# W_2's product of a 1-core transformer block, swept stage by stage over both column pairs, with its operands in a ring of four places on GpSimd's queue

## The chip, the core and the metric

One Trainium2 chip; the kernel is one program on one of its cores. The metric is the device time of one execution in microseconds. A core has TensorE (PE; its weight loads are shown as PEld), VectorE (DVE), ScalarE (ACT), GpSimd (POOL) and SyncE (SP), which issues DMAs from its queue. Matmuls read their operands from SBUF and write to PSUM; the large arrays lie in DRAM.

## What is computed

One transformer layer on 512 tokens of width 2048, in float32: an input layer norm, a combined projection, pooling and stick-breaking attention, an output projection with a residual and a layer norm, then the part that the change is about:

```python
h = layer_norm(DEEPNORM_ALPHA * h + mix, ln1_g, ln1_b)
f = jnp.einsum('bsd,df->bsf', h, w_ff1) + b_ff1        # 512 x 2048 by 2048 x 8192
f = jnp.square(jax.nn.relu(f))
f = jnp.einsum('bsf,fd->bsd', f, w_ff2) + b_ff2        # 512 x 8192 by 8192 x 2048
h = layer_norm(DEEPNORM_ALPHA * h + f, ln2_g, ln2_b)
```

## The kernel before, in words

Each float32 product is made of three fast matmuls: an operand is split into a high part (a cast) and a low part (operand minus high part), and `three` (L286) adds high by high, high by low and low by high in one PSUM bank.

**Phase 1, W_1's product.** It runs over 16 blocks of 512 columns of d_ff (`product`, L198). A block has eight groups; for each, `weights` (L191) loads 512 KB of W_1 on SP's queue and `parts_of` (L179) forms the high and low parts, on ACT and DVE, a half at a time in four places. A group is 24 matmuls, a block 192. The product comes out in four PSUM banks. `operands` (L684) takes them: ACT adds the bias and applies relu (r), DVE squares into g (L692), and three more DVE steps make sums (L696). The second product uses Strassen's scheme in Winograd's form, and its seven left operands, A11, A12, A22 and S1 to S4, are these sums of quarters of the block. One cast (L700) makes all seven high parts, one subtraction (L701) the seven low parts, and two writes of 1792 KB on SP's queue (L703) store them in DRAM (fh_d, fl_d), in rows of 2 KB. One place holds the high parts, one the low parts.

**Phase 2, W_2's product.** It has 4 slices (NS) of 4 blocks (PER). `load_ops` (L716) loads a slice's seven operands, high and low, 1 MB each, 14 MB in all, on SP's queue into 14 places of the pool left. W_2 is read in units of 512 KB (`w2_unit`, L727; a ring of five), and `parts` (L734) forms the parts of a unit or of a sum of units in a ring of three. `columns` (L756) does the seven products of one slice for one pair of column quarters n and n + 2: stage 1 is A11 by b11 into banks x, and S1 by c = b12 - b11 into banks v; stage 2 is S2 and S4 by b22 - c and b22; stage 3 is S3 by b22 - b12; stage 4 is A12 and A22 by b21 and b21 - c. A stage runs over four units u, and a product of one unit is 12 matmuls (`times`, L741). After each stage `accumulate` (L749) adds the banks into acc, where the residual and the bias already stand. So a slice is 7 x 4 x 2 x 12 = 672 matmuls: n = 0 with all its stages, then n = 1. In the last half slice A22's product comes last, behind `between`, which loads the last layer norm's vectors into old operand places and normalises the first two of the four row blocks (`norm_out`, L821); the other two follow at the end.

The order on each engine comes from a list scheduler, which places instructions of a `high_priority` region some steps ahead; loads and parts stand in such regions.

## Time and profile before

| | us |
|---|---|
| runs (median, lowest, highest) | 2037.07, 2036.92, 2039.73 |
| the profiled execution, its own time | 2033.09 |
| its span | 2031.4 |
| TensorE busy, share of the span | 1934.5, 95% |
| DVE busy | 1238.1, 61% |
| ACT busy | 766.3, 38% |
| POOL busy | 25.6, 1% |

The span is that of the instructions of one execution. A wait is idle time of an engine, put down to what released it. The granted clock is that of TensorE as a share of its full speed of 2.4 GHz; 0.5 is its lower level, 1.2 GHz. GB/s is what the core's 16 DMA engines moved, and the DMA share is the mean busy share of these. The last two phases of the program are W_1's product (to about 1326 us) and W_2's (from there to 2004 us).

### The profile page before, as it was taken

Reading aid. Unit: us, or ns where it says so; the run is one execution under the profiler, and the core shown is the slowest. Engines: PE = TensorE matmul, PEld = TensorE weight load, DVE = VectorE, ACT = ScalarE, POOL = GpSimd, SP = SyncE. Lnnn points to the kernel's source line nnn. Section 1 sums busy time; section 2 is a strip of 40 time slices with the busy share of each in tenths; the row PEclk is TensorE's granted clock in tenths of the full one; section 3 lists DMA queues with packets and bytes.
Section 4 is the critical chain, followed back from the end, with each engine's and each line's share of the span. In section 5 each row is a group of like instructions: output and inputs, shape, how many; then the busy total and the mean of one; then the engine's idle time right before and its main releaser. Section 6 shows DMA issues by size and latency. Waiting matters only on the chain.

```text
span 2031.4 us, 22728 instructions
## 1 busy us (share of the span) xinstructions
PE 1934.5 (95%) x8736; PEld 1594.1 (78%) x8736; DVE 1238.1 (61%) x1697; ACT 766.3 (38%) x1082; POOL 25.6 (1%) x42
## 2 busy tenths in 40 slices
PE   5999999999999999999999999938999999999994
PEld 4888888888889888888888888826788788778773
DVE  8445565775469444544444544435877777877878
ACT  3354655642234233333333333322333333333331
POOL 5000000000000000000000000000000000000000
PEclk9999999999999999999999999968999999999997
DMA  5132222235344354565544565477596587587552
GB/s 218 32 94 74 82 86 81 74 117 184 106 148 126 138 166 166 205 208 170 172 166 166 206 207 171 141 292 288 166 357 246 176 331 266 182 311 281 178 186 83
DMA packets 170156, 358.07 MB, mean 176 GB/s; under 512 B 9792, under 2 KB 27328, under 8 KB 162496
## 3 DMA queue, kind: packets, MB, share of 16 engines
q1 hardware_dynamic: 169904, 356.55, 50.5%
q8 instruction: 68, 1.11, 0.2%
q14 instruction: 40, 0.33, 0.0%
q10 hardware_dynamic: 144, 0.07, 0.0%
HBM read 293.67 MB, written 62.91 MB: 176 GB/s over the span
## 4 chain that ended last, share of the span: by engine, by line
PE 77%; DMA 12%; DVE 9%; issue 1%; ACT 1%; SPq 0%; DVEq 0%; ACTq 0%
PE f L214 32%; PE qk L367 9%; PE x L289 7%; PE o L214 7%; DMA b<-in_w_ff_dram 6%; PE v L289 5%; PE p L214 4%; DMA b12b<-in_w_ff_dram 4%; PE o L289 3%; DVE tl L738 2%; PE v L214 2%; PE f L289 2%; PE w L289 2%; DVE acc L751 1%; DVE c L769 1%; DMA o3l<-fl_d 1%
## 5 line engine op out<-in xcount | busy, mean ns | idle before, releaser
L214 PE MATMUL f<-h1l,wh_f 128*128 128x512 f32 x960 | 373.5, 389 | 0.0
L214 PE MATMUL f<-h1h,wh_f 128*128 128x512 f32 x960 | 371.2, 389 | 0.0
L214 PE MATMUL f<-h1h,wl_f 128*128 128x512 f32 x960 | 353.8, 389 | 0.3 <-DVE wl_f L186 0.3
L186 DVE TENSOR_TENSOR wl_f<-raw_f,wh_f 128x512 fp32r<-128x512 f32 x240 | 160.2, 689 | 307.2 <-ACT wh_f L185 261.4
L185 ACT CAST wh_f<-raw_f 128x512 fp32r<-128x512 f32 x240 | 146.0, 621 | 407.7 <-PE f L214 395.1
L214 PEld LDWEIGHTS f<-h1h,wl_f 128*128 128x128 f32 x960 | 180.2, 188 | 38.0 <-DVE wl_f L186 0.7
L214 PEld LDWEIGHTS f<-h1l,wh_f 128*128 128x128 f32 x960 | 180.3, 188 | 37.4
L214 PEld LDWEIGHTS f<-h1h,wh_f 128*128 128x128 f32 x960 | 180.2, 188 | 37.3
L737 ACT CAST th<-c 128x1024 fp32r<-128x1024 f32 x96 | 101.2, 1054 | 189.2 <-PE x L289 57.2
L737 ACT CAST th<-b 128x1024 fp32r<-128x1024 f32 x96 | 101.2, 1054 | 170.9 <-PE x L289 112.5
L738 DVE TENSOR_TENSOR tl<-b,th 128x1024 fp32r<-128x1024 f32 x96 | 117.1, 1220 | 43.3 <-ACT th L737 42.9
L738 DVE TENSOR_TENSOR tl<-c,th 128x1024 fp32r<-128x1024 f32 x96 | 117.2, 1220 | 39.1 <-ACT th L737 39.0
L367 PE MATMUL qk<-hTl,wh_qk 128*128 128x512 f32 x256 | 99.8, 390 | 0.0
L367 PE MATMUL qk<-hTh,wh_qk 128*128 128x512 f32 x256 | 99.5, 390 | 0.0
L367 PE MATMUL qk<-hTh,wl_qk 128*128 128x512 f32 x256 | 98.8, 390 | 0.0
L701 DVE TENSOR_TENSOR fl<-g,fh 128x3584 fp32r<-128x3584 f32 x16 | 62.3, 3893 | 40.2 <-ACT fh L700 40.2
L186 DVE TENSOR_TENSOR wl_qk<-raw_qk,wh_qk 128x512 fp32r<-128x512 f32 x64 | 43.9, 688 | 64.4 <-ACT wh_qk L185 62.1
L214 PE MATMUL o<-wh_o,mixl 128*128 128x512 f32 x192 | 76.0, 396 | 0.0
L214 PE MATMUL o<-wl_o,mixh 128*128 128x512 f32 x192 | 75.9, 395 | 0.0
L289 PE MATMUL x<-th,o0h 128*128 128x512 f32 x128 | 46.4, 401 | 29.9 <-DMA o0h<-fh_d 28.7
L214 PE MATMUL o<-wh_o,mixh 128*128 128x512 f32 x192 | 72.9, 395 | 0.0
L769 DVE TENSOR_TENSOR c<-b,b 128x1024 f32<-128x1024 f32 x32 | 39.1, 1221 | 38.6 <-DMA b<-in_w_ff_dram 38.6
(236 smaller groups left out, 3914.9 us busy)
## 6 DMA issues: line engine op xcount, KB each, us to landing
b<-in_w_ff_dram SPq DMA_DIRECT2D x128, 512.0 KB, 5.0
raw_f<-in_w_ff_dram SPq DMA_DIRECT2D x120, 512.0 KB, 3.8
fh_d<-fh SPq DMA_DIRECT2D x16, 1792.0 KB, 6.0
fl_d<-fl SPq DMA_DIRECT2D x16, 1792.0 KB, 7.3
raw_qk<-in_w_in_dram SPq DMA_DIRECT2D x64, 256.0 KB, 2.9
b22b<-in_w_ff_dram SPq DMA_DIRECT2D x32, 512.0 KB, 4.1
b12b<-in_w_ff_dram SPq DMA_DIRECT2D x32, 512.0 KB, 4.5
raw_o<-in_w_out_dram SPq DMA_DIRECT2D x24, 512.0 KB, 3.7
```

Of the source, the lines that this page charges most:

```text
L185: nc.scalar.copy(h, raw[:, i, :])
L186: nc.vector.tensor_tensor(l, raw[:, i, :], f(h), op=ALU.subtract)
L214: mm = nc.tensor.matmul(bank, a, b, start=first and n == 0, stop=last and n == 2)
L289: mm = nc.tensor.matmul(bank, l, r, start=first and n == 0, stop=last and n == 2, skip_group_check=free)
L367: nc.tensor.matmul(bank, a, b, start=kc == 0 and n == 0, stop=kc == KC - 1 and n == 2)
L701: nc.vector.tensor_tensor(l, full, f(h), op=ALU.subtract)
L737: nc.scalar.copy(h, t)
L738: nc.vector.tensor_tensor(l, t, f(h), op=ALU.subtract)
L751: nc.vector.tensor_tensor(acc[tb0 + t][q], acc[tb0 + t][q], bank, op=ALU.add)
L769: nc.vector.tensor_tensor(c, b12, b11, op=ALU.subtract)
```

## The change

- `parts_of` forms the parts of a whole group (two rows of weights) by one cast and one subtraction, in two places instead of four of half the size. The pool of the weights, wp, now lives to the end.
- `operands` works in two halves of 128 of the 256 rows: each half has its cast, its subtraction and two writes of 896 KB in rows of 1 KB, on GpSimd's queue in place of SP's. A single place of half the size holds the high parts, another the low parts, so the second half's cast waits until the first half's write has landed.
- Operands of phase 2 are loaded on GpSimd's queue, a pair (high, low) at a time, into a ring of four places: two of the pool first, which is opened before phase 1 and lives on, and two of the pool right. The pairs come in order A11, S1, S2, S4, S3, A12, A22 and then those of the next slice.
- `slice_of` takes the place of `columns`: each stage runs over both column pairs before the next one, so an operand is used for both and then given up. Both pairs' c (eight of 512 KB) stay for the slice, banks are x0, x1, v0, v1, and raw units and parts come alternately from wp and right.
- The last layer norm's two vectors are loaded by two transfers (1 MB each) when `norm_out` is first reached in the order of the program, into places of their own; the first two row blocks' normalisation stands after all of w, ahead of A22's products. The second pair's A22 product is written a row block at a time.
- Spare loads of `resident` in an earlier part are one transfer of 512 KB in place of two of 256 KB.

```diff
-        wh, wl = [], []
-        for i in range(GK):
-            h = wp.tile([P, N], F32R, tag="wh", bufs=4, name=f"wh_{name}_{i}")
-            l = wp.tile([P, N], F32R, tag="wl", bufs=4, name=f"wl_{name}_{i}")
-            nc.scalar.copy(h, raw[:, i, :])
-            nc.vector.tensor_tensor(l, raw[:, i, :], f(h), op=ALU.subtract)
...
+        h = wp.tile([P, GK, N], F32R, tag="wh", bufs=2, name=f"wh_{name}")
+        l = wp.tile([P, GK, N], F32R, tag="wl", bufs=2, name=f"wl_{name}")
+        nc.scalar.copy(h, raw)
+        nc.vector.tensor_tensor(l, raw, f(h), op=ALU.subtract)
...
+    first = pool(ctx, "first", 2, side="right")
     staging = early.enter_context(ExitStack())
...
-        full = g[:, :OPS].rearrange("p o i t -> p o (i t)")
-        h = stage.tile([P, OPS, N], F32R, tag="h", name=f"fh{b}")
-        l = stage.tile([P, OPS, N], F32R, tag="l", name=f"fl{b}")
-        nc.scalar.copy(h, full)
-        nc.vector.tensor_tensor(l, full, f(h), op=ALU.subtract)
-        for d, t in ((fh_d, h), (fl_d, l)):
-            nc.sync.dma_start(d[b // PER][:, :, b % PER, :].rearrange("o p n -> p o n"), f(t))
+        for i in range(2):
+            full = g[:, :OPS, i, :]
+            h = stage.tile([P, OPS, H2], F32R, tag="h", name=f"fh{b}_{i}")
+            l = stage.tile([P, OPS, H2], F32R, tag="l", name=f"fl{b}_{i}")
+            nc.scalar.copy(h, full)
+            nc.vector.tensor_tensor(l, full, f(h), op=ALU.subtract)
+            for d, t in ((fh_d, h), (fl_d, l)):
+                nc.gpsimd.dma_start(d[b // PER][:, :, b % PER, i * H2:(i + 1) * H2].rearrange("o p t -> p o t"), f(t))
...
+    def operand(s, o):
+
+        pl = right if turn("op", 2) else first
+        both = []
+        for d, n in ((fh_d, "h"), (fl_d, "l")):
+            t = pl.tile([P, PER, 2, H2], F32R, tag=f"o{n}", bufs=2, name=f"o{n}{s}_{o}")
+            nc.gpsimd.dma_start(f(t), d[s][o].rearrange("p u (i t) -> p u i t", i=2))
+            both.append(t)
+        return both
...
+        raw = (right if turn("raw") else wp).tile([P, 2, N], F32, tag="raw", bufs=3, name=name)
...
+        with ahead():
+            S3 = operand(s, 5)
+        for n in range(2):
+            for u in units:
+                b, at, e = s * PER + u, f"{s}_{n}_{u}", (False, u == PER - 1)
+                with ahead():
+                    b22 = w2_unit(b, 1, n + 2, f"b22b_{at}")
+                    b12 = w2_unit(b, 0, n + 2, f"b12b_{at}")
+                    nc.vector.tensor_tensor(b22, b22, b12, op=ALU.subtract)
+                    p7 = parts(b22, f"7_{at}")
+                times(x[n], S3, u, p7, *e)
+            accumulate(x[n], 2, n + 2)
...
         if end:
...
+            for tb in range(2):
+                norm_out(tb)
+            for u in units:
+                times(x[0], A22, u, fourth(0, u), False, u == PER - 1)
+            accumulate(x[0], 2, 0)
+            p4 = [fourth(1, u) for u in units]
+            for t in range(2):
+                for u in units:
+                    times(x[1], A22, u, p4[u], False, u == PER - 1, (t,))
+                accumulate(x[1], 2, 1, (t,))
+                norm_out(2 + t)
```

How the change moves the instructions is shown at three places. A row has the line, the operation, the tiles and the semaphores that it waits on: DMAHW those of transfers from SP's queue, DMASW those from GpSimd's, the others of engines.

In a block of W_1's product, DVE's order; g, fl are the block's operands, wl_f the low parts of the next block's weights, with the group's first row in the name. Before:

```order
L696 TENSOR_TENSOR g_10036<-g_10036 128x512 [waits DVE_49] x3
L186 TENSOR_TENSOR wl_f_0_4_0_10134<-raw_f_0_4_10131,wh_f_0_4_0_10133 128x512 [waits DMAHW2_49,PE_49,Activation_49]
L701 TENSOR_TENSOR fl_10054<-g_10036,fh_10053 128x3584 [waits DMAHW4_49,Activation_49]
L186 TENSOR_TENSOR wl_f_0_4_1_10138<-raw_f_0_4_10131,wh_f_0_4_1_10137 128x512 [waits PE_49,Activation_49]
L186 TENSOR_TENSOR wl_f_0_6_0_10168<-raw_f_0_6_10165,wh_f_0_6_0_10167 128x512 [waits DMAHW3_49,PE_49,Activation_49]
```

And of the change:

```order
L691 TENSOR_TENSOR g_8255<-g_8255 128x512 [waits DVE_49] x3
L184 TENSOR_TENSOR wl_f_0_4_8351<-raw_f_0_4_8348,wh_f_0_4_8350 128x1024 [waits DMAHW2_49,PE_49,Activation_49]
L697 TENSOR_TENSOR fl_0_8273<-g_8255,fh_0_8272 128x1792 [waits DMASW3_49,Activation_49]
L184 TENSOR_TENSOR wl_f_0_6_8381<-raw_f_0_6_8378,wh_f_0_6_8380 128x1024 [waits DMAHW3_49,PE_49,Activation_49]
L697 TENSOR_TENSOR fl_1_8279<-g_8255,fh_1_8278 128x1792 [waits DMASW5_49,Activation_49]
L184 TENSOR_TENSOR wl_f_0_8_8411<-raw_f_0_8_8408,wh_f_0_8_8410 128x1024 [waits DMAHW4_49,PE_49,Activation_49]
```

The low parts are formed in two halves, and the second one waits for a write of the same block, with wl_f_0_8 behind it.

At the change of phase, SP's queue, which brings W_2's units (b) and, before, the operands (o0h is A11's high part). Before:

```order
L195 DMA raw_f_0_14_10301<-in_w_ff_dram 128x2x512 [waits DMAHW4_49,DVE_49]
L703 DMA fh_d_5845<-fh_10352 128x7x512 [waits Activation_49]
L703 DMA fl_d_5849<-fl_10353 128x7x512 [waits DVE_49]
L731 DMA b_0_0_0_10407<-in_w_ff_dram 128x2x512 [waits PE_49]
...
L722 DMA o0h_10373<-fh_d_5842 128x2048 [waits DMAHW1_49,PE_49]
L722 DMA o0l_10375<-fl_d_5846 128x2048 [waits PE_49]
```

And of the change, where the third number of a b is its unit u:

```order
L191 DMA raw_f_0_14_9590<-in_w_ff_dram 128x2x512 [waits DMAHW4_49,DVE_49]
L730 DMA b_0_0_0_9676<-in_w_ff_dram 128x2x512 [waits DMAHW5_49,DVE_49]
...
L730 DMA b_0_0_2_9754<-in_w_ff_dram 128x2x512
L852 DMA ln2g<-in_ln_g_dram 128x2048 [waits DMASW4_49,DMASW2_49,DMASW6_49,DMASW0_49,DVE_49]
L852 DMA ln2b<-in_ln_b_dram 128x2048 [waits DMASW5_49,DMASW7_49,DMASW3_49,DMASW1_49]
L730 DMA b_0_0_3_9790<-in_w_ff_dram 128x2x512 [waits DMAHW0_49,DVE_49]
```

Writes and operands have left this queue, six units stand right behind W_1's last load, and the last layer norm's vectors stand ahead of unit 3, with waits for writes on GpSimd's queue.

In the same place DVE's order in the change; tl is the low part of a unit or of a c, and TensorE's order is x0 with units 0 to 2, then v0 with units 0 to 2:

```order
L691 TENSOR_TENSOR g_9620<-g_9620 128x512 [waits DVE_49] x3
L738 TENSOR_TENSOR tl_0_0_2_9757<-b_0_0_2_9752,th_0_0_2_9756 128x1024 [waits DMAHW2_49,Activation_49]
L697 TENSOR_TENSOR fl_0_9638<-g_9620,fh_0_9637 128x1792 [waits DMASW7_49,Activation_49]
L697 TENSOR_TENSOR fl_1_9644<-g_9620,fh_1_9643 128x1792 [waits DMASW1_49,Activation_49]
L775 TENSOR_TENSOR c_0_0_9684<-b_0_0_0_9678,b_0_0_0_9676 128x1024 [waits DMAHW3_49]
L775 TENSOR_TENSOR c_0_1_9722<-b_0_0_1_9716,b_0_0_1_9714 128x1024 [waits DMAHW4_49]
```

Parts of the first three units (two of them ahead of these rows) are formed before the last block's low parts; the first c stands behind both of these.

## Rows read from the trace of the kernel before

**Rows 1.** Stretches: us; busy PE, PEld, DVE, ACT, POOL; granted clock, DMA share, GB/s.

```profile
75.00:1325.60 1250.60, 1250.31 (x5805) 1043.62 (x5803) 656.11 (x1046) 492.90 (x769) 0.00 (x0) 1.00 0.43 142
1325.60:1400.00 74.40, 34.35 (x107) 24.11 (x106) 31.43 (x30) 15.62 (x14) 0.00 (x0) 0.70 0.84 339
...
1453.20:1608.80 155.60, 154.41 (x673) 125.59 (x673) 120.01 (x116) 58.98 (x56) 0.00 (x0) 1.00 0.71 257
...
1920.20:2004.20 84.00, 78.83 (x337) 63.75 (x336) 66.58 (x79) 27.80 (x28) 0.00 (x0) 0.98 0.36 122
2004.20:2031.40 27.20, 0.16 (x1) 0.00 (x0) 23.08 (x52) 0.48 (x2) 0.00 (x0) 0.57 0.43 155
```

**Rows 2.** Waits of TensorE, after 1320 us, and in W_1's product (the last row).

```profile
PE x L289 <- DMA o0h<-fh_d: 28.7, 1, 28.7
PE x L289 <- DVE tl L738: 6.6, 7, 2.4
...
PE f L214 <- DVE wl_f L186: 0.3, 1, 0.3
```

**Rows 3.** Timeline of engines at the change of phase: start us, us, engine, line.

```profile
1324.63 2.19 ACT L689 ACTIVATE r<-f,vecT 128x512 f32<-128x512 f32 x3
1325.56 0.39 PE L214 MATMUL f<-h1h,wl_f 128*128 128x512 f32 x1
1330.18 3.18 ACT L700 CAST fh<-g 128x3584 fp32r<-128x3584 f32 x1 [3.36 <-DVE g L696]
1333.39 3.89 DVE L701 TENSOR_TENSOR fl<-g,fh 128x3584 fp32r<-128x3584 f32 x1 [3.25 <-ACT fh L700]
1337.72 5.40 SPq L731 DMA_DIRECT2D b<-in_w_ff_dram  x5
1343.22 0.50 SPq L722 DMA_DIRECT2D o0h<-fh_d  x1
1354.67 0.77 PE L289 MATMUL x<-th,o0h 128*128 128x512 f32 x1 [28.72 <-DMA o0h<-fh_d]
...
DMA to landing us min/median/max: 11.3/11.3/11.3
```

**Rows 4.** The page's groups of instructions: casts and low parts of phase 2.

```profile
L737 ACT CAST th<-b 128x1024 fp32r<-128x1024 f32 x96 | 101.2, 1054 | 170.9 <-PE x L289 112.5
L738 DVE TENSOR_TENSOR tl<-b,th 128x1024 fp32r<-128x1024 f32 x96 | 117.1, 1220 | 43.3 <-ACT th L737 42.9
L769 DVE TENSOR_TENSOR c<-b,b 128x1024 f32<-128x1024 f32 x32 | 39.1, 1221 | 38.6 <-DMA b<-in_w_ff_dram 38.6
```

**Rows 5.** ACT's timeline in a block of W_1's product, and in the next one.

```profile
1149.87 2.20 ACT L689 ACTIVATE r<-f,vecT 128x512 f32<-128x512 f32 x3 [0.28 <-PE f L214]
...
1193.39 2.20 ACT L689 ACTIVATE r<-f,vecT 128x512 f32<-128x512 f32 x3 [0.28 <-PE f L214]
```

**Rows 6.** The stretch 1355 to 1375, with the columns of rows 1.

```profile
1355.00:1375.00 20.00, 15.54 (x45) 10.53 (x45) 3.24 (x3) 2.09 (x2) 0.00 (x0) 0.76 1.02 424
```

**Rows 7.** The page's DMA issues: count, KB each, us to landing.

```profile
raw_f<-in_w_ff_dram SPq DMA_DIRECT2D x120, 512.0 KB, 3.8
fh_d<-fh SPq DMA_DIRECT2D x16, 1792.0 KB, 6.0
fl_d<-fl SPq DMA_DIRECT2D x16, 1792.0 KB, 7.3
```

**Rows 8.** DVE's timeline in the tail.

```profile
1993.02 1.28 DVE L751 TENSOR_TENSOR acc<-acc,w 128x512 f32<-128x512 f32 x2
...
2007.44 1.27 DVE L751 TENSOR_TENSOR acc<-acc,x 128x512 f32<-128x512 f32 x2
...
2010.37 5.32 DVE L829 SCALAR_TENSOR_TENSOR acc<-acc,rs_n,ln 128x512 f32<-128x512 f32 x8
```

**Rows 9.** DVE's groups from 700 to 1300 us, by form.

```profile
L186 DVE TENSOR_TENSOR wl_f<-raw_f,wh_f 128x512 fp32r<-128x512 f32 x221 | 147.7, 689 | 286.5 <-ACT wh_f L185 242.4 <-PE f L214 44.1
L701 DVE TENSOR_TENSOR fl<-g,fh 128x3584 fp32r<-128x3584 f32 x14 | 54.5, 3893 | 33.7 <-ACT fh L700 33.7
```

More of the change, by code (lines that the diff above doesn't have):

```diff
@@ L797, in columns @@
-        p4s = []
-        for u in range(PER):
-            b = s * PER + u
-            with ahead():
-                b21 = w2_unit(b, 1, n, f"b21_{s}_{n}_{u}")
-                p2 = parts(b21, f"2_{s}_{n}_{u}")
-                c = chain[u]
-                nc.vector.tensor_tensor(c, b21, c, op=ALU.subtract)
+        units = range(PER)
+        x = [pair(f"x{s}_{n}", f"x{n}") for n in range(2)]
+        v = [pair(f"v{s}_{n}", f"v{n}") for n in range(2)]
+        chain = {}
+        with ahead():
+            A11, S1 = operand(s, 0), operand(s, 3)
@@ new lines, in slice_of @@
+        with ahead():
+            S2, S4 = operand(s, 4), operand(s, 6)
+        for n in range(2):
+            for u in units:
+                b, at, e = s * PER + u, f"{s}_{n}_{u}", (False, u == PER - 1)
+                with ahead():
+                    b22 = w2_unit(b, 1, n + 2, f"b22_{at}")
+                    c = chain[n, u]
+                    nc.vector.tensor_tensor(c, b22, c, op=ALU.subtract)
+                    p6 = parts(c, f"6_{at}")
+                    p3 = parts(b22, f"3_{at}")
+                times(x[n], S2, u, p6, *e)
+                times(v[n], S4, u, p3, *e)
+            accumulate(x[n], 0, n + 2)
+            accumulate(v[n], 0, n + 2)
@@ new lines, in slice_of, with second, fourth @@
+        with ahead():
+            A12, A22 = operand(s, 1), operand(s, 2)
+        w = [pair(f"w{s}_{n}", f"v{n}") for n in range(2)]
+        def second(n, u):
+            at = f"{s}_{n}_{u}"
+            with ahead():
+                b21 = w2_unit(s * PER + u, 1, n, f"b21_{at}")
+                c = chain[n, u]
+                nc.vector.tensor_tensor(c, b21, c, op=ALU.subtract)
+                p2 = parts(b21, f"2_{at}")
+            times(w[n], A12, u, p2, u == 0, u == PER - 1)
+        def fourth(n, u):
+            with ahead():
+                return parts(chain[n, u], f"4_{s}_{n}_{u}")
@@ L805, in columns @@
+        for n in range(2):
+            for u in units:
+                second(n, u)
                 if not end:
[L806 to L807 removed]
+                    times(x[n], A22, u, fourth(n, u), False, u == PER - 1)
+            accumulate(w[n], 0, n)
             if not end:
[L809 to L810 removed]
+                accumulate(x[n], 2, n)
         if end:
[L812 to L816 removed]
```

146 lines of the change are left out of this document (50 added, 96 removed).

## The prediction

> **What bounds the kernel now.** I read the stretches first, then the waits of TensorE, then the rows around the change of phase, and last the DVE rows of the tail. In the table of stretches [rows 1] TensorE is busy 1250.31 of 1250.60 us during W_1's product and 154.41 of 155.60 in a full slice of W_2's: in both it is the bound, at a granted clock of 1.00. Three places leave it idle. From 1325.6 to 1400.0, the change of phase, it is busy 34.35 of 74.40 us at a mean clock of 0.70. The last half slice takes 84.00 us for 337 matmuls. And the last 27.20 us hold one matmul, while DVE is busy 23.08. A slice gives the price of a matmul: 155.60 / 673 = 0.231 us with its small stalls, and 0.227 without (one block of W_1, 192 matmuls, repeats after 1193.39 - 1149.87 = 43.52 us [rows 5]). So the 107 matmuls of the change of phase are 107 x 0.227 = 24.3 us of work, and 50.1 of its 74.4 us are lost.
>
> The waits say on what: one of 28.7 us on the load of the first operand, while nothing of the kind stands in W_1's product, whose only wait of TensorE is 0.3 us [rows 2]. The chain behind the 28.7 us [rows 3]: ACT evicts the last block, rounds all seven operands in one cast of 3.18 us, DVE forms the low parts in 3.89, the two 1792 KB writes go to SP's queue, then five loads of W_2, and only behind these, at 1343.22, the load of A11, which lands 11.3 us later. After it TensorE waits again and again: over 1355 to 1375 the DMA engines are at a share of 1.02 and 424 GB/s [rows 6], since 14 MB of operands and the first W_2 units arrive at once. The rest of the 50.1 us is the clock: TensorE's 34.35 busy us are 10.0 over 24.3.
>
> **The change, part by part.** I work with the profiled execution of before: 2033.09 us, of which 2031.4 are the span and 1.7 lie around it. It is 4.0 us under the median of the runs shown, 2037.07; I add those 4.0 at the end.
>
> *The change of phase.* Slice 0's A11 and S1 are now loaded on GpSimd's queue right after block 3's writes, over 500 us early, into places that phase 1 doesn't use; W_2's first six units are asked for ahead of the last block's operands. So the 28.7 us wait loses its cause. Let T be the end of the last W_1 matmul, about 1325.8 [rows 3]. The parts of the first unit are formed before T, and TensorE runs x0 with units 0 to 2: 36 x 0.227 = 8.2 us, to about T + 9. What is late next is c_0_0, S1's other factor. On DVE it stands behind fl_0 and fl_1, and fl_1 now waits until fl_0's write has landed, since the two halves share one place. Before, the cast began 4.4 us after T; two W_2 parts now stand ahead of it, so T + 5.3. Half a cast is 1.6 us, half of fl 1.95: fl_0 is written at T + 8.9. With L for the landing time of such a write, fl_1 is done at T + 10.9 + L, c_0_0 (1.2) at T + 12.1 + L, its cast (1.05) [rows 4] at T + 13.2 + L. TensorE stands idle for 4.2 + L.
>
> L is in no row: nothing of before is written from GpSimd's queue, and no write has 896 KB. Below, a 512 KB load lands in 3.8 us; above, I double fl_d's 7.3 us for 1792 KB to 14.6, because the queue is another one. I take 6.0, the landing of fh_d [rows 7], which has the same 896 rows at twice the length, as the nearest row. The Trainium skill ("DMA: Bandwidth & Descriptors", section on the anatomy of one DMA on the GpSimd path) fits 2.0 us plus the bytes over 436 GB/s, which would be an estimate of 4.1 us and make the sum 2 us lower; no row here shows that queue.
>
> So the idle time is 10.2 us. Then S1 with units 0 to 2 runs 8.2 us, and the next units are late: the two ln2 loads stand on SP's queue ahead of unit 3 and wait for fl_1's landing, near T + 11 + 2 x 6 = T + 23; they bring 2 MB, and S2 and S4 bring 4 MB at the same time, of which a W_2 unit gets a share of 424 GB/s. I take 5.5 us, between 0 (the loads get ahead) and 15 (6 MB at 424 GB/s, all of it in the way). The clock: before, it cost 10.0 over many idle stretches; I see two that remain and take 2.3, between 0 and 10.0. The start takes 0.8. In all 0.8 + 10.2 + 5.5 + 2.3 = 18.8 us are lost in place of 50.1: **-31**. From the bounds of L alone the loss is 16.6 to 27.4; with those of loads and clock it is 9 to 45, so the term reaches from -41 to -5.
>
> *Full slices.* The products are the same 672 matmuls, DVE and ACT work the same: DVE is busy 120 of 155.6 us. 3.3 us above 672 x 0.2267 = 152.3 are lost in each, and the change touches that with opposite signs: operand loads move off SP's queue, but S3's stage now asks two units, 1 MB, per 2.72 us for 8 units running, 385 GB/s, beside 4 MB of the next operands. Behind it three raw places of a kind hold back some of it. I take 0, between -2 and +5 per slice, -8 to +20 for four.
>
> *The end.* The last half slice's 84.0 us are 6.1 over 337 x 0.231 = 77.9. Its operands and parts are now all asked for in the same ring as elsewhere: -4, between 0 and -6. In the tail all of w is finished first, then 96 matmuls are left in place of 48. Before, the last w was added at 1993.02, 38.4 us ahead of the end [rows 8]. Now DVE has 25.0 us of queued work from the end of w to the addition of the last x (12 additions and statistics of 0.635 us, 7.6; five low parts of 1.22, 6.1; 16 scaling operations of 0.665, 10.6; 0.7 for the small ones), TensorE 21.8. From that addition before takes 2031.4 - 2007.44 = 24.0 us, of which 5.3 are eight scalings that now stand ahead of it: 18.6. So the end comes 43.6 us after w, 5.2 later than now, but w ends 48 x 0.227 = 10.9 earlier: **-5.5**, between -11 (DVE's queue is hidden) and 0.
>
> *Phase 1.* Fused parts save DVE and ACT some fixed cost, both well under TensorE: 0. Operand writes lie beside W_1's matmuls: 0 as long as L is short. That is the place to look at. In a block, t from its first matmul, some 1.2 us after the r row [rows 5], as at the change of phase [rows 3]: the operands g are ready near t = 6, fh_0 at 7.7, fl_0 at 9.7. Behind fl_1 on DVE stands wl_8, of which the fifth group has need at 4 x 5.44 + 0.45 = 22.2. fl_1 and wl_8 take 3.1 us, so fl_0 must have landed at t = 19.1: L may be 9.4 us. On ACT, fh_1 and wh_8 stand likewise, with more room. The spare loads of one DMA in place of two: 0, since they stand in a stretch with a DMA share of 0.43 or less.
>
> Sum: -31 - 4 - 5.5 = -40.5, so 1992.6 us by the profiled execution, and **1997** beside the median of before.
>
> **Rivals.** *Writes land late (slower).* If L passes 9.4 us, ACT and DVE hold back TensorE in each of the 15 blocks that have a product beside them, at (L - 9.4) us a block, and L - 6 us at the change of phase. The gain of 40.5 is gone where 15(L - 9.4) + (L - 6) = 40.5, at L = 11.7; at 14.6 the kernel would need 78 + 8.6 - 40.5 = 46 us more than before, 2083. For it: a block's 3584 KB now go in four writes of 1 KB rows, 3584 rows in place of 1792, on a queue that no row of before shows. Against it: fh_d's 6.0 and fl_d's 7.3 us for twice the bytes, and a DMA share of 0.43. What DVE runs in W_1's product is subtractions and products of two inputs, above all 221 of wl_f and 14 of fl in 600 us [rows 9]. The Trainium skill ("SBUF — State Buffer", the section on two separate sides) warns that a DMA from GpSimd's queue can starve, because GpSimd writes its descriptors itself and is shut out while DVE runs in a two-port mode, of which an fp32 copy is the example; by that rule this change is the wrong way round and L would grow by what DVE holds. Neither of these rows is a copy, so the trace gives it little weight. I give the rival 0.17, which is mostly the unknown queue.
>
> *W_2 starves.* The ring of four operand places, or stage 3's loads, cost 5 us or more a slice: 2015 to 2033. For it: 424 GB/s is what the trace shows at most, and 385 is near it. Against: that is only 21.8 us of a slice of 155.6, and the mean was 257 GB/s. 0.15.
>
> *The phase change hardly shortens.* If A11's early load waits for something of phase 1 after all, or the ln2 loads block SP's queue for long, 10 us remain of 31: 2018 to 2035, with the end's gain. 0.05.
>
> **How the numbers follow.** Forecast 0.60 (1984 to 2015), better than that 0.03, starved 0.15, unshortened 0.05, late writes 0.17. The change that this kernel's measurement can just tell is 0.2%, 4 us. All but the late writes end below 2033, save a part of the unshortened: faster 0.79, same 0.04, slower 0.17. The range from 1983 to 2035 leaves the late writes out, and the little below.
>
> **What would show it.** Right: TensorE's wait on the first operand is gone and its next waits are on th of c and on W_2 units; the loss around 1325 to 1380 is near 19 us; the slices stay near 155.6; the landing times on GpSimd's queue are 4 to 9 us; W_1's blocks stay 43.5 us long. Wrong: blocks longer than 43.6, with waits on wl_f or wh_f near the fifth group; or x waits on S3's parts in each slice; or TensorE's wait at the change of phase is still on an operand.

## The result, and the profile after

The changed kernel takes **2028.17 us** (median; 2023.15 to 2029.64) beside 2036.92 (2035.42 to 2039.73) of the kernel before in the same runs: a ratio of 0.995, interval 0.9934 to 0.9965. It is faster by 9 us, where 40 were forecast.

| | before | after |
|---|---|---|
| the profiled execution, its own time | 2033.09 | 2028.36 |
| its span | 2031.4 | 2026.7 |
| last W_1 matmul starts | 1325.56 | 1328.44 |
| first W_2 matmul starts | 1354.67 | 1329.07 |
| last W_2 matmul starts | 2003.97 | 2005.61 |

Taken apart, the span is shorter by 4.7 us: 2.9 later up to the last W_1 matmul, 28.5 less from there to the first W_2 matmul, **27.2 more from the first W_2 matmul to the last**, and 6.3 less behind it. So the wait that the change was aimed at is gone, and nearly all of it came back inside W_2's product.

The stretches of the kernel after, with the columns of rows 1 (us; busy PE, PEld, DVE, ACT, POOL; granted clock, DMA share, GB/s). The first two and the last answer to [rows 1], the third to [rows 6]; 1516.58 to 1678.40 is slice 1, 1721.92 and 1773.16 begin the stages 2 and 3 of slice 2, and the row of 15 us lies in slice 0's stage 3:

```profile
75.00:1328.50 1253.50, 1251.28 (x5804) 1043.98 (x5802) 639.00 (x864) 468.01 (x587) 58.90 (x64) 1.00 0.45 147
1328.50:1400.00 71.50, 50.29 (x196) 38.40 (x195) 47.75 (x47) 23.15 (x22) 6.99 (x10) 0.86 0.69 259
1355.00:1375.00 20.00, 9.53 (x33) 6.89 (x32) 6.22 (x6) 3.35 (x4) 0.00 (x0) 0.74 1.02 406
...
1516.58:1678.40 161.82, 156.75 (x674) 125.69 (x673) 119.09 (x117) 58.80 (x56) 7.34 (x14) 1.00 0.69 247
...
1721.92:1773.16 51.24, 46.52 (x193) 37.09 (x192) 30.50 (x30) 16.79 (x16) 2.10 (x4) 0.97 0.60 209
1773.16:1800.52 27.36, 23.28 (x97) 17.66 (x96) 19.18 (x20) 8.00 (x8) 1.05 (x2) 1.00 0.93 351
...
1445.00:1460.00 15.00, 13.01 (x54) 9.64 (x52) 8.07 (x10) 1.95 (x2) 0.00 (x0) 1.00 1.02 415
...
2005.50:2026.70 21.20, 0.50 (x3) 0.07 (x1) 17.30 (x37) 0.48 (x2) 0.00 (x0) 0.57 0.52 185
```

A full slice has become 161.82 us from 155.60. Stage 3 needs 27.36 us for 96 matmuls, 21.8 at 0.2267 each (a block of W_1: 43.52 / 192), with the DMA engines at a share of 0.93; in slice 0's stage 3 the share is 1.02 at 415 GB/s, the level of [rows 6]. Stage 2 of this slice takes 51.24 for 43.5.

The waits of TensorE after 1320 us, which answer to [rows 2]:

```profile
PE x L283 <- ACT th L737: 21.0, 7, 10.4
PE v L283 <- ACT th L737: 10.5, 1, 10.5
PE v L283 <- DVE tl L738: 6.9, 2, 4.7
PE x L283 <- DVE tl L738: 4.8, 9, 1.5
PE w L283 <- DVE tl L738: 0.4, 1, 0.4
```

The 28.7 us on an operand are gone. In their place are two waits of 10.4 to 10.5 us, both at the change of phase, and some 23 us on parts of W_2 units in the slices. The change of phase in the timeline of the kernel after, which answers to [rows 3]:

```profile
1328.44 0.39 PE L210 MATMUL f<-h1h,wl_f 128*128 128x512 f32 x1
...
1329.07 0.51 PE L283 MATMUL x<-th,oh 128*128 128x512 f32 x1 [0.25 <-ACT r L684]
...
1334.20 1.70 ACT L696 CAST fh<-g 128x1792 fp32r<-128x1792 f32 x1 [0.97 <-DVE g L691]
...
1338.59 0.94 POOL L699 DMA_DIRECT2D fl_d<-fl  x1 [1.46 <-DVE fl L697]
...
1344.11 2.03 DVE L697 TENSOR_TENSOR fl<-g,fh 128x1792 fp32r<-128x1792 f32 x1 [6.16 <-DMA fl_d<-fl]
1346.06 2.35 DVE L775 TENSOR_TENSOR c<-b,b 128x1024 f32<-128x1024 f32 x2
...
1348.41 1.22 PE L283 MATMUL v<-th,oh 128*128 128x512 f32 x2 [10.46 <-ACT th L737]
...
1351.69 0.34 SPq L852 DMA_DIRECT2D ln2b<-in_ln_b_dram  x1
1352.14 13.33 SPq L730 DMA_DIRECT2D b<-in_w_ff_dram  x6
...
1368.68 1.04 ACT L737 CAST th<-b 128x1024 fp32r<-128x1024 f32 x1 [13.79 <-DMA b<-in_w_ff_dram]
1369.78 1.22 PE L283 MATMUL x<-th,oh 128*128 128x512 f32 x2 [10.43 <-ACT th L737]
```

The first wait is the chain that the prediction worked out: fl_1 waits for fl_0's write, c for fl_1, S1's product for c. The second is unit 3, whose load is issued at 1352.14, behind the last layer norm's vectors. The DMA issues of the kernel after, which answer to [rows 7]:

```profile
fh_d<-fh POOLq DMA_DIRECT2D x32, 896.0 KB, 5.3
fl_d<-fl POOLq DMA_DIRECT2D x32, 896.0 KB, 5.9
oh<-fh_d POOLq DMA_DIRECT2D x28, 1024.0 KB, 7.9
...
b22b<-in_w_ff_dram SPq DMA_DIRECT2D x32, 512.0 KB, 6.3
```

Last, slice 2's stage 2, the timeline of the kernel after (the matmuls between are left out):

```profile
1730.32 0.39 PE L283 MATMUL v<-th,oh 128*128 128x512 f32 x1
...
1733.02 1.22 DVE L789 TENSOR_TENSOR c<-b,c 128x1024 f32<-128x1024 f32 x1 [8.20 <-DMA b<-in_w_ff_dram]
1734.16 1.22 DVE L738 TENSOR_TENSOR tl<-b,th 128x1024 fp32r<-128x1024 f32 x1
...
1735.43 0.80 PE L283 MATMUL v<-tl,oh 128*128 128x512 f32 x1 [4.72 <-DVE tl L738]
```

TensorE is without work from 1730.32 to 1735.43 for want of a tl. The b of that tl had landed before 1730 (its high part was cast at 1727.72). But DVE works in order, and a c for a later product, whose unit came late, stood ahead of it.

### The profile page after: what moved, and what is told of

It is laid out like the page before. It is cut to its first block, busy times and chain, and to the rows that moved or that the text cites. A ratio compares the mean times of both kernels' runs of the same rounds, so it can differ in the third digit from the quotient of the medians.

```text
span 2026.7 us, 22165 instructions
## 1 busy us (share of the span) xinstructions
PE 1940.9 (96%) x8736; PEld 1595.6 (79%) x8736; DVE 1216.1 (60%) x1513; ACT 739.4 (36%) x898; POOL 115.4 (6%) x162
## 4 chain that ended last, share of the span: by engine, by line
PE 53%; issue 23%; DVE 10%; DMA 10%; POOL 2%; ACT 1%; SPq 0%; DVEq 0%; POOLq 0%; ACTq 0%
PE f L210 9%; PE qk L361 9%; PE x L283 6%; PE o L210 6%; DMA b<-in_w_ff_dram 5%; PE p L210 4%; PE v L283 4%; DVE tl L738 4%; DMA b22b<-in_w_ff_dram 4%; PE o L283 3%; PE w L283 3%; PE f L283 2%; PE v L210 2%; POOL fh_d L699 1%; POOL fl_d L699 1%
## 5 line engine op out<-in xcount | busy, mean ns | idle before, releaser
L184 DVE TENSOR_TENSOR wl_f<-raw_f,wh_f 128x1024 fp32r<-128x1024 f32 x120 | 146.8, 1224 | 276.3 <-ACT wh_f L183 276.3
L183 ACT CAST wh_f<-raw_f 128x1024 fp32r<-128x1024 f32 x120 | 126.4, 1053 | 361.4 <-PE f L210 320.9
L283 PE MATMUL x<-th,oh 128*128 128x512 f32 x512 | 195.8, 397 | 21.2 <-ACT th L737 21.0
L283 PE MATMUL x<-tl,oh 128*128 128x512 f32 x512 | 203.9, 398 | 5.2 <-DVE tl L738 4.8
L283 PE MATMUL x<-th,ol 128*128 128x512 f32 x512 | 202.0, 394 | 0.0
L283 PEld LDWEIGHTS x<-tl,oh 128*128 128x128 f32 x512 | 96.9, 189 | 33.3 <-DVE tl L738 12.0
L283 PEld LDWEIGHTS x<-th,ol 128*128 128x128 f32 x512 | 96.9, 189 | 21.3
L283 PE MATMUL v<-th,oh 128*128 128x512 f32 x256 | 98.9, 398 | 10.5 <-ACT th L737 10.5
L283 PE MATMUL v<-tl,oh 128*128 128x512 f32 x256 | 102.3, 400 | 6.9 <-DVE tl L738 6.9
L283 PE MATMUL v<-th,ol 128*128 128x512 f32 x256 | 101.7, 397 | 0.0
```

The lines of the kernel that those rows point to most:

```text
L183: nc.scalar.copy(h, raw)
L184: nc.vector.tensor_tensor(l, raw, f(h), op=ALU.subtract)
L283: mm = nc.tensor.matmul(bank, l, r, start=first and n == 0, stop=last and n == 2, skip_group_check=free)
```

## The experiments

**How they are read.** The loss of a stage is the time from its first matmul's start to that of the next stage, less 0.2267 us for each matmul between. A stage is counted in TensorE's order by its number of matmuls in a slice (192, 192, 96 and 192). The loss is worked out from the starts in each run's one profiled execution. "Start" is slice 0's first 96 matmuls (x0 and v0 of stage 1); the other columns are sums over the four slices. The kernel before has 19.7 in the start, behind the 28.7 us wait, and 20.4 elsewhere. The runs of one kernel lie up to 14 us apart (e1_align: 2022.38 to 2036.02), so a difference of a few us between two variants tells nothing unless the intervals part.

| variant | median, us | ratio to before | start | stage 1 | stage 2 | stage 3 | stage 4 |
|---|---|---|---|---|---|---|---|
| the change | 2028.17 | 0.995 (0.9934 to 0.9965) | 26.5 | 2.0 | 11.6 | 22.4 | 4.9 |
| e1_align | 2030.06 | 0.9965 (0.9952 to 0.9979) | 27.4 | 2.3 | 5.3 | 21.4 | 4.9 |
| e5_align256 | 2032.06 | 0.9961 (0.9949 to 0.9973) | 26.3 | 4.1 | 12.5 | 25.3 | 1.3 |
| e3_chain | 2023.74 | 0.9934 (0.9916 to 0.9952) | 25.0 | 2.0 | 11.5 | 17.0 | 2.7 |
| e6_a11late | 2024.9 | 0.9926 (0.9906 to 0.9946) | 26.4 | 2.0 | 6.6 | 18.8 | 3.8 |
| e8_chain_late | 2028.8 | 0.9945 (0.9928 to 0.9961) | 26.9 | 2.0 | 4.8 | 3.8 | 26.6 |
| e12_spread | 2024.43 | 0.9934 (0.9913 to 0.9955) | 23.0 | 1.9 | 13.2 | 21.0 | 3.0 |
| e14_rows2k | 2038.22 | 1.0001 (0.9991 to 1.0011) | 25.5 | 6.6 | 12.9 | 31.5 | 4.6 |
| e17_sp_ops | 2018.11 | 0.9897 (0.9883 to 0.9911) | 25.9 | 2.0 | 2.7 | 24.6 | 3.8 |
| e4_lnlate | 2027.96 | 0.9956 (0.9942 to 0.9969) | 20.2 | 2.0 | 10.5 | 30.7 | 3.6 |
| e15_lag4 | 2033.11 | 0.9971 (0.9958 to 0.9984) | 27.3 | 1.9 | 2.7 | 35.1 | 3.6 |
| e7_all | 2029.51 | 0.9959 (0.9941 to 0.9977) | 7.8 | 15.3 | 14.3 | 13.5 | 26.6 |
| e13_all2 | 2013.39 | 0.9876 (0.9858 to 0.9894) | 8.5 | 5.9 | 24.8 | 7.2 | 15.3 |
| e16_all_lag4 | 1971.92 | 0.967 (0.9656 to 0.9683) | 6.6 | 8.5 | 0.0 | 0.6 | 0.4 |
| e16_all_lag6 | 1969.9 | 0.9658 (0.9643 to 0.9672) | 10.4 | 1.0 | 0.0 | 0.0 | 0.0 |

A stage's loss also moves where nothing in the stage was edited. In stage 2 the change and the six variants that leave its loads and its order alone (e1, e5, e3, e6, e8, e4) have 4.8 to 12.5; in stage 3 the change, e1 and e5 have 21.4 to 25.3. Most variants of the change that were expected to gain came out slower than their theory said, by up to 40 us (e7); both e16 came out over 10 us faster.

### Is it the matmuls themselves?

In the slices of the change, matmuls with operands in the two places of the pool first follow each other at 233 ns, those of the pool right at 227. As the kernel is built, first's places begin 224 bytes past a multiple of 256 bytes of a partition, right's at a multiple of 256. Four edits moved such a beginning. **e1_align** and **e5_align256** move first's places in the change, e1 by 96 bytes as here, e5 by 224 with `[P, 56]`:

```diff
+    pool(ctx, "gap", 1, side="right").tile([P, 24], F32, tag="gap", name="gap")
     first = pool(ctx, "first", 2, side="right")
```

> The change, with 96 unused bytes a partition ahead of the pool first, so that its two operand places start at a multiple of 128 bytes; now they start at 96 past one. Nothing else moves. Theory (a place that starts off 128 bytes makes each matmul that takes its stationary operand from it slower, 233 ns from start to start in place of 227): all of W_2's matmuls run at 227 ns, about 1340 of 2688 gain 6.7 ns each, 9 us, so near 2019 us. Rival (the slow matmuls go with the side, the queue or the time at which the place is loaded): 233 ns stays for the operands of first, and the time stays near 2028.

> The change, with 224 unused bytes a partition ahead of the pool first, so that its two operand places start at a multiple of 256 bytes. In the run with a multiple of 128, which is not one of 256, the operands of first stayed at 233 ns a matmul; the fast places of both kernels start at multiples of 256. Theory (multiple of 256 is what counts): the matmuls with operands of first fall to 227 ns, 9 us of TensorE's time in all, of which some goes into waits, so 2019 to 2025. Rival (it is where the pool lies, above 192 KB): they stay at 233 and the time at 2028.

e1 (a multiple of 128 but not of 256) still has 11.16 us per 48 matmuls with first's operands, 232.5 ns: the theory of 128 bytes falls. e5 (a multiple of 256) has 227. The same piece, three quarters of slice 2's stage 2 (144 matmuls), in the stretches of the change:

```profile
1739.56:1773.16 33.60, 33.60 (x145) 27.02 (x144) 21.84 (x21) 12.60 (x12) 1.05 (x2) 1.00 0.51 165
```

And of e5:

```profile
1739.99:1772.63 32.64, 32.64 (x146) 27.04 (x144) 20.73 (x20) 12.66 (x12) 1.05 (x2) 1.00 0.56 186
```

33.60 / 144 is 233.3 ns, 32.64 / 144 is 226.7. **e2_shift** is the converse, in the kernel before: all operands of phase 2 move by 32 bytes (and the tiles that lie behind them by 128).

```diff
+    pool(late, "gap0", 1).tile([P, 8], F32, tag="gap0", name="gap0")
     left = pool(late, "left", 1)
+    pool(late, "gap1", 1).tile([P, 24], F32, tag="gap1", name="gap1")
     right = pool(late, "right", 1)
```

> The kernel before, with its 14 operand places moved up by 32 bytes a partition, and all other tiles of phase 2 kept at multiples of 128. Theory of the start address: all 2688 matmuls of W_2's product go from 227 to 233 ns, so 18 us more than before, some 2055. Rival (the address has no part): unchanged, 2037.

Its matmuls go to 233.3 ns, and its median is 2045.8, a ratio of 1.0047 (1.0031 to 1.0064). 2688 matmuls by 6.6 ns are 17.7 us, and the small waits of a slice gave way for part of them: slice 1 takes 157.4 us, of which 156.8 are 672 x 0.2333. **e11_before_slots** moves, in the kernel before, a pool of the earlier part from 64 past a multiple of 256 to a multiple; in it lie the stationary tiles of the output projection and those of W_1's block 0:

```diff
+    slots.tile([P, 48], F32, name="gap_s")
```

> The kernel before, with 192 unused bytes a partition in the pool slots, so that the tiles of the earlier part that follow start at multiples of 256 bytes instead of 64 past one. Nothing else. Theory of the start address: the matmuls of the output projection, at 231 to 235 ns from about 440 to 625 us, fall to 227, so 4 to 5 us less: some 2032 against 2037. Rival: no change.

The last W_1 matmul starts at 1322.64, 2.9 us earlier, the median is 2034.91 and the ratio 0.9984 (0.9975 to 0.9993). The output projection's 768 matmuls go from 233.3 to 226.8 ns, 5.0 us less. But the 384 of block 0, which have 256 columns, go the other way, from 113.8 to 119.8 ns, 2.3 us more. So the effect is real, though not one rule for every shape. And it isn't what costs in the change: e5 has every matmul of W_2 at 227 and is no faster. The 9 us that it saves (half of the 2688 matmuls, 6.6 ns each) are waits in its profiled execution: by the table it loses 69.5 us in all, the change 67.4.

### Is it the bandwidth of stage 3?

**e3_chain** forms b22 - b12 as c - b11, since c = b22 - (b12 - b11) lies in SBUF already: one unit is loaded per product in place of two.

```diff
-                    b22 = w2_unit(b, 1, n + 2, f"b22b_{at}")
-                    b12 = w2_unit(b, 0, n + 2, f"b12b_{at}")
-                    nc.vector.tensor_tensor(b22, b22, b12, op=ALU.subtract)
...
+                    b11 = w2_unit(b, 0, n, f"b11b_{at}")
+                    nc.vector.tensor_tensor(b11, chain[n, u], b11, op=ALU.subtract)
```

> The change, with stage 3's factor b22 - b12 formed as c - b11, c being what stage 2 leaves (b22 - b12 + b11): one unit of 512 KB is loaded for it in place of two, 16 MB less in all, with as many DVE and ACT operations. Theory (the stalls of TensorE in stage 3, some 5 to 7 us a slice, are its loads, 1 MB for 2.72 us of matmuls, that meet 4 MB of operand loads at the limit of the DMA engines): stage 3 loses under 1.5 us a slice, 18 us less in all, near 2010. Rival (the stalls come from the ring of three raw places or the parts' ring, whatever the bytes): under 6 us gained, over 2022.

**e6_a11late** holds the load of the next slice's A11 until this slice's stage 3 has ended:

```diff
-            A11, S1 = operand(s, 0), operand(s, 3)
+            A11, S1 = operand(s, 0, ended.get(3)), operand(s, 3)
```

> The change, with the load of the next slice's A11 held back until the last matmul of stage 3. Theory (stage 3 asks 8.4 MB of units and 4.2 MB of operands, 577 GB/s over its 21.8 us, where 424 is what the DMA engines have given): with 2.1 MB less the stalls there fall from 5 to 7 us a slice to 2 to 4, so some 2017 to 2022. Rival (the stalls are the ring of raw places): no change there.

**e8_chain_late** has both edits.

> Both edits on stage 3 together: its factor formed as c - b11, with one unit in place of two, and the next A11 held back until its end. Theory: 4.2 + 2.1 MB in 21.8 us, 289 GB/s; stage 3 loses under 1 us a slice above the 233 ns matmuls, so some 2010 to 2015. Rival: a stall of 3 us or more a slice is left, from the burst of A22's load or the ring, near 2020.

e3 and e6 each take some us out of stage 3 (22.4 to 17.0 and 18.8), though neither total can be told from the change's; together, in e8, they leave 3.8. So stage 3 does ask for more than comes: less data, or the same data a little later, and its loss goes. But e8's total is that of the change, since each of the first three stages 4 now loses 8.6 to 9.4 us. The stretches of e8's slice 2, stages 3 and 4:

```profile
1771.03:1793.98 22.95, 22.07 (x97) 17.94 (x96) 17.65 (x19) 8.44 (x8) 0.00 (x0) 1.00 0.66 230
1793.98:1846.17 52.19, 46.69 (x194) 37.50 (x192) 33.25 (x33) 16.81 (x16) 3.15 (x6) 0.93 0.61 210
```

A mean of 210 GB/s is far below the 415 further up: no shortage over the stage, but a burst, since A11 held back and S1 come at once. DVE waited 6.5 us for one unit of a c there, and TensorE 5.5 for a low part.

**e12_spread** holds back A11, S1, S4 and A12, each to the end of half a stage, so that one pair comes at a time:

```diff
-            A11, S1 = operand(s, 0), operand(s, 3)
+            A11, S1 = operand(s, 0, done_mm.get((3, 1))), operand(s, 3, done_mm.get((4, 0)))
...
-            A12, A22 = operand(s, 1), operand(s, 2)
+            A12, A22 = operand(s, 1, done_mm[2, 0]), operand(s, 2)
```

> The change, with each pair of operands (2.1 MB) held back by a dependency on TensorE's progress, so that no two pairs are asked for at once: S4 waits for the first column pair's stage 1, A12 for its stage 2, A11 for the end of stage 3, S1 for the first column pair's stage 4. Same bytes, queues and places. Theory (two pairs at once, 4.2 MB, take the DMA engines for 10 us from W_2's units, and TensorE stalls behind a late unit): the stalls at the starts of stages 2 and 4 vanish, 2 to 4 us stay in stage 3, where 8.4 + 2.1 MB in 21.8 us are still 481 GB/s; 10 to 15 us less, some 2013 to 2018. Rival (the bytes alone set the stalls, however they are spread): 2024 to 2028.

It gains little, 21.0 us are lost in stage 3, and it is not told from the change.

**e14_rows2k** brings an operand in four transfers with rows of 2 KB, to see whether the length of rows sets how the two queues share the engines:

```diff
-            nc.gpsimd.dma_start(f(t), d[s][o].rearrange("p u (i t) -> p u i t", i=2))
+            for u in range(PER):
+                nc.gpsimd.dma_start(f(t)[:, u], d[s][o][:, u].rearrange("p (i t) -> p i t", i=2))
```

> The change, with each operand load cut into four of 256 KB, a unit each, so that its rows are 2 KB like those of W_2's units, in place of 8 KB. Same bytes and queue. Theory (the DMA engines serve the two queues row by row, so an operand load with 8 KB rows gets four times the share of a unit with 2 KB rows): units land sooner while operands are loaded, stalls of stages 2 to 4 fall by a third or more, 2015 to 2022. Rival (the engines share by bytes, or are just full): no change, 2025 to 2030, or a little slower by the added issues on GpSimd.

It is 10 us slower than the change (intervals apart), with 31.5 in stage 3: that theory falls. Which of the edit's two sides costs, the shorter rows or the fourfold transfers, is not shown.

**e17_sp_ops** loads the operands on SP's queue again:

```diff
-            nc.gpsimd.dma_start(f(t), d[s][o].rearrange("p u (i t) -> p u i t", i=2))
+            nc.sync.dma_start(f(t), d[s][o].rearrange("p u (i t) -> p u i t", i=2))
```

> The change, with the operand loads of phase 2 on SP's queue, where those of the kernel before were; ring, places and writes as changed. Theory (a second queue lets a pair of operands take the DMA engines from units that were asked for earlier; on one queue they go in order, but an operand load that waits for its place holds up the units behind it): within 8 us of the change, either way, 2020 to 2036, with other stalls: fewer late units, and waits of the queue on TensorE. Rival (the queue itself costs): 15 us or more faster.

It is 10 us faster than the change (intervals apart): stage 2's loss is 2.7 in place of 11.6, the start's and stage 3's stay. The stretch of its stage 3 in slice 2 still has a DMA share of 0.94:

```profile
1766.21:1795.66 29.45, 24.65 (x98) 19.42 (x97) 21.46 (x21) 7.97 (x8) 0.00 (x0) 0.88 0.94 344
```

So two costs were mixed: the second queue, some 10 us, and the amount of data in stage 3, which this choice of queue doesn't mend. In slice 2's stage 2 the landings show what differs. In e17 the transfers there land in the order in which they were asked for. In the change a unit is asked for at 1721.32, ahead of the high part of a second pair (1722.15), and lands behind it, at 1732.99 against 1731.85. That is the unit for whose c DVE waits in the timeline above. The row of DMA issues for it alone, and then for the same unit in e1_align, whose operands are on GpSimd's queue too and which asked for it 1.6 us earlier, beside the first pair:

```profile
b<-in_w_ff_dram SPq DMA_DIRECT2D x1, 512.0 KB, 11.7
b<-in_w_ff_dram SPq DMA_DIRECT2D x1, 512.0 KB, 6.5
```

So the same unit on the same two queues is late or not by a small shift in time, and e1's stage 2 loses 5.3 us without e17's edit. That the choice of queue makes the 10 us is shown; that it makes all 9 us of stage 2 is not. The Trainium skill ("DMA: Bandwidth & Descriptors", section on queues, rings and completion order) states that each DMA engine takes turns between the queues that have work for it. By that rule operands on a second queue take turns with a unit already asked for; the landings agree with it, and no run measured the shares.

### Is it the layer norm's vectors, at the change of phase?

**e4_lnlate** puts the vectors into places of first that phase 2 gives up late:

```diff
-                t = gb[n] = right.tile([P, NQ, N], F32, tag=f"ln2{n}", bufs=1, name=f"ln2{n}")
+                t = gb[n] = first.tile([P, NQ, N], F32, tag="oh" if n == "g" else "ol", bufs=2, name=f"ln2{n}")
```

> The change, with the last layer norm's two vectors loaded into an old operand place of first, which comes free in the last slice; so their loads leave SP's queue at the change of phase. Theory (the second idle stretch there, 10.8 us, is unit 3 waiting behind these loads on SP's queue, which wait for the last operand writes): the stretch shrinks to 3 to 5 us and the time to about 2021. Rival (it is S2's and S4's 4 MB, issued at once on GpSimd's queue, that fill the DMA engines): the stretch stays at 8 us or more and the time at 2025 to 2028.

The loads are now issued from 1931.95 on, in slice 3. The second wait of TensorE falls from 10.4 to 4.3 us, and the start's loss by 6.3. The total doesn't move: the loads now stand in slice 3's stage 3, whose loss goes from 3.2 to 9.9. In both places units stand behind the vectors on SP's queue, and the vectors cost some 6 us.

### Is it DVE's order?

**e15_lag4** makes each difference of units wait for the end of the product four before:

```diff
+    def minus(o, x, y):
+        ins = nc.vector.tensor_tensor(o, x, y, op=ALU.subtract)
+        if len(seq) >= 4:
+            after(ins, seq[-4])
...
-                    nc.vector.tensor_tensor(c, b12, b11, op=ALU.subtract)
+                    minus(c, b12, b11)
```

> The change, with each difference of W_2 units on DVE held back until the matmuls four products (10.9 us) ahead of its use are done; no byte and no place moves. Theory (TensorE's stalls of 2 to 6 us in the slices are DVE waiting in order for a unit that is needed much later, with low parts that are needed now behind it): the stalls at the starts of stage 2 vanish (14 us in the profiled run of the change's slices 2 and 3, less in others), stage 3's shrink a little; some 2015 to 2021. Rival (the units that stall TensorE are themselves late): no change, 2025 to 2030.

This keeps a difference for a later product from standing ahead of low parts for the next one. Stage 2's loss is 2.7 in place of 11.6, below that of every variant that leaves the stage alone: waits there were of DVE's order behind a late unit, as in the timeline above, though not all of the 9 us need be (e1 has 5.3). But stage 3's rises from 22.4 to 35.1, and the total is no better. The stretches of e15's stages 2 and 3 in slice 2:

```profile
1728.23:1773.03 44.80, 44.80 (x194) 35.99 (x193) 34.03 (x33) 16.81 (x16) 2.10 (x4) 1.00 0.59 210
1773.03:1803.98 30.95, 24.54 (x98) 19.25 (x96) 19.96 (x20) 8.31 (x8) 1.05 (x2) 0.89 0.96 348
```

As I read it, working ahead had cost low parts in stage 2 and saved them in stage 3, where the same data come however DVE is ordered.

### All of it together

**e7_all** and **e13_all2** form the parts of phase 1 in halves again, start first and slots at multiples of 256, take stage 3 from c - b11, load the vectors behind the last stage 3, and form the last block's second half on GpSimd. e7 holds back A11, A12 and, in slice 0, S2 and S4; e13 spreads the pairs as e12 does. Of e13:

```diff
+            last = i and b == BLOCKS - 1
+            (nc.gpsimd.tensor_copy if last else nc.scalar.copy)(h, full)
+            (nc.gpsimd if last else nc.vector).tensor_tensor(l, full, f(h), op=ALU.subtract)
...
+                dma = nc.sync.dma_start(t, vec.rearrange("(q n) -> q n", n=N).partition_broadcast(P))
+                after(dma, done_mm[3, 1])
```

> A version meant to beat both: places of first and of the earlier part's slots at multiples of 256; stage 3 from c - b11; A11 and A12 held back, slice 0's S2 and S4 held back until its first column pair has run stage 1; the last layer norm's loads after the last stage 3; weight parts formed in halves again; and the last block's second half formed on GpSimd, so that ACT and DVE don't wait for the first half's write. By the theory each of these takes away a measured loss: 9 (addresses in W_2) + 4 (addresses in the earlier part) + 18 (stage 3) + 14 to 18 (the two idle stretches at the change of phase) + 3 (halves) + 6 (stalls at the starts of stage 2), 50 us off 2028, so 1980 to 1990. If the causes are wrong in the main, over 2005.

> The version meant to beat both, mended: multiples of 256 for first and slots, weight parts in halves, stage 3 from c - b11, operands spread one pair at a time as in the run beside it (in the earlier version S2 and S4 came late together, and A11 and S1 at once), the last layer norm's loads after the last stage 3, and the last block's second half on GpSimd. Theory: no stall over 1.5 us in the slices, some 15 us lost at the change of phase in place of 27, 6 us less before it: 1985 to 1995. Rival (waits on W_2's units come back elsewhere): 2010 or more.

e7 gains nothing over the change: S2 and S4, held back, come late together, and slice 0's stage 1 loses 15.3 us beside them; stage 4 loses 26.6 as in e8. e13 is at 0.9876, with stage 3 down to 7.2, but stage 2 at 24.8 and stage 4 at 15.3. The timeline of e13 in slice 1's stage 2 shows why:

```profile
1576.40 0.39 PE L285 MATMUL v<-th,oh 128*128 128x512 f32 x1
...
1577.60 1.23 DVE L811 TENSOR_TENSOR b11b<-c,b11b 128x1024 f32<-128x1024 f32 x1 [4.12 <-DMA b11b<-in_w_ff_dram]
...
1579.34 1.22 DVE L745 TENSOR_TENSOR tl<-b,th 128x1024 fp32r<-128x1024 f32 x1
...
1580.61 0.80 PE L285 MATMUL v<-tl,oh 128*128 128x512 f32 x1 [3.82 <-DVE tl L745]
```

DVE waits for a unit of stage 3, which begins at 1595.56 there, while TensorE waits for a tl behind it. **e16_all_lag4** and **e16_all_lag6** are e13 with the hold of e15, of four and of six products; of the latter:

```diff
-                    nc.vector.tensor_tensor(b11, chain[n, u], b11, op=ALU.subtract)
+                    minus(b11, chain[n, u], b11)
```

> The mended version of all edits, with the same hold of DVE's differences. Theory: its stalls in the middle of stages 2 and 4, 4 to 8 us each, seven in the profiled run, are this order on DVE; they vanish, 30 us less, so some 1983 to 1992. Rival: 2008 to 2015 as without.

> As the run beside it, with the hold at six products, 16.3 us. Theory: between the version without a hold and the one with four products, near the latter; 1983 to 1998.

These waits are gone. The stretches of e16_all_lag6 in slice 2, its four stages:

```profile
1639.70:1683.22 43.52, 43.52 (x193) 36.06 (x192) 32.94 (x33) 16.87 (x16) 2.10 (x4) 1.00 0.73 257
1683.22:1726.74 43.52, 43.52 (x193) 36.06 (x192) 35.47 (x35) 16.85 (x16) 2.10 (x4) 1.00 0.58 206
1726.74:1748.50 21.76, 21.76 (x97) 18.03 (x96) 19.40 (x20) 8.44 (x8) 0.00 (x0) 1.00 0.75 272
1748.50:1792.02 43.52, 43.52 (x193) 36.07 (x192) 32.47 (x32) 16.87 (x16) 3.14 (x6) 1.00 0.64 223
```

Each stage is its matmuls' 0.2267 us and nothing else, and the DMA share of stage 3 is 0.75 in place of 0.93. Its waits of TensorE after 1320 us are those of the change of phase alone:

```profile
PE v L285 <- DVE tl L752: 3.5, 2, 3.0
PE v L285 <- ACT th L751: 2.3, 1, 2.3
PE x L285 <- ACT th L751: 0.7, 1, 0.7
```

At 1969.9 us (1966.91 to 1970.91) it is 3.4% faster than the kernel before, and beats both. The effects don't add: the hold alone (e15) gains nothing over the change, the rest alone (e13) is at 0.9876, both together at 0.9658. Holds of four and six are the same within their intervals. How much of the last step each part of e13 carries was not tried one by one.

## Why the prediction was off, point by point

The direction and the range were right, the size was not: 8.7 us faster in place of 40. By the steps of the sum, from the profiled executions (0.1 us is left by rounding):

| step | predicted | came |
|---|---|---|
| change of phase, with the first 192 matmuls of W_2 | -31 | -23.2 |
| full slices | 0 | +25.2 |
| the end (the last 336 matmuls) | -4 | -3.2 |
| tail | -5.5 | -6.3 |
| phase 1 | 0 | +2.9 |

**Full slices: this is the step that failed.** It said: "I take 0, between -2 and +5 per slice", and 25.2 us came, over the +20 that it allowed for four slices. The two numbers that decide stood in one sentence of it, 385 GB/s for the units of stage 3 "beside 4 MB of the next operands", and were not added. 16 units of 524 KB are 8.4 MB, two operand pairs 4.2 MB; in 96 x 0.2267 = 21.8 us that is 577 GB/s, against the 424 of [rows 6]. At 424 the same 12.6 MB need 29.7 us, 8 more than the matmuls have, less what units in hand cover: 7.2, 6.4 and 5.6 were lost in stage 3 of slices 0 to 2, 19.2 us in all. With less data and a later A11, e8 loses 3.8 over all four slices. The operands are A22 and the next A11: in slice 0 GpSimd issues them from 1440.84 to 1444.61, and stage 3 begins at 1443.33. The rival that W_2 starves named this case, 2015 to 2033 us, and the time fell into it; it got 0.15 because the mean over a slice (257 GB/s) was held against it. A mean says nothing of a stage of 22 us with six raw places. Other costs in the slices stood in no step: DVE's order and the second queue, which both bear on stage 2 (2.7 us in e15 and e17 in place of 11.6, though e1, with neither edit, has 5.3), and the 233 ns matmuls, 2.2 us a slice, which the prediction took at 227. The prediction read DVE's order at the change of phase but not in a slice.

**Change of phase: right in kind, 8 us off in size.** The 28.7 us wait went, and the next waits are those named, on th of c and on unit 3. The first is 10.46 us, predicted 10.2, with landing times of 5.3 and 5.9 us for L = 6.0. The second was put at 5.5, between 0 and 15, and is 10.43. Unit 3's load was issued when the prediction said, 23.7 us after the last W_1 matmul (T + 23), but its data were there only at 1368.7, 16.5 us later, beside the vectors' and S2's and S4's 6 MB: the stretch from 1355 to 1375 has a share of 1.02 at 406 GB/s, as before [rows 6]. e4 shows that the vectors made 6.1 us of the wait. The clock was put at 2.3: from 1328.5 to 1400 TensorE is busy 50.29 us for 196 matmuls, 44.4 at 0.2267, at a granted clock of 0.86, so it was 5.9, about 1 of it from the 233 ns matmuls.

**The end and the tail: right.** (The tail's own terms, 5.2 later and 10.9 earlier, give -5.7, not -5.5.) DVE's last addition of x in the timeline of the kernel after, which answers to [rows 8]:

```profile
2008.45 1.28 DVE L752 TENSOR_TENSOR acc<-acc,x 128x512 f32<-128x512 f32 x2
```

From there to the end of the span, 2026.7, it takes 18.2 us, predicted 18.6.

**Phase 1: the writes cost nothing, as forecast, and the fused parts did cost.** TensorE is busy 1251.28 of 1253.50 us up to the last W_1 matmul, with no wait in W_1's product. The rival that writes land late falls with the landing times, far below its 9.4 us. The starving that the Trainium skill warns of ("SBUF — State Buffer", two separate sides) is not seen; DVE ran subtractions and products of two inputs beside these writes, no copy of the kind that the warning names, so this case doesn't try that rule. The estimate of 4.1 us for such a write from the Trainium skill's fit ("DMA: Bandwidth & Descriptors", anatomy of one DMA) is below the medians of 5.3 and 5.9, in which other traffic is included. Matmul by matmul TensorE falls behind by 3.0 us between 444 and 455 us; over the rest of the way the difference moves by 0.6 us at most. There it has three waits, 2.2 us in all, that before doesn't have, with slow steps beside them: 1.1 on a fused low part of o's weights (wl_o), and 0.9 and 0.2 on yh and yl beside it. e16_all_lag6, with halves again, doesn't wait on wl_o, and 0.7 in all on the others.

## What to carry to other kernels

Add up what a stage asks of the DMA engines, units and operands and everything that the ring's freed places set off, and divide by that stage's own time, before taking a mean over the loop for comfort. An engine that works in order must not be given work far ahead whose data may be late, when work for the next product stands behind it; here holding such work back paid only together with the cuts and shifts of data (e16), not alone (e15), and a cure alone may show nothing. A large transfer moved to a second queue to be out of the way still uses the same engines as the small ones that are waited for.
